# Turning gated blocks by a transposing DMA that reads from DRAM, in a fused retention and window-attention layer

## The chip, the cores and the metric

The kernel runs on one core of a Trainium2 chip. The metric is the device time of one execution in microseconds (us), the median of several runs. Besides the timed runs there is one execution with the hardware profiler on; its page and its trace are what this document reads. The granted TensorE clock was 1.000 over the whole profiled execution.

## What is computed

One decoder layer on x of 2048 tokens by 1024 channels, all in float32. One input projection makes 2816 columns; two groups of heads run side by side, their gated outputs are joined and projected back.

```python
h = rms_norm(x, norm_w)
proj = h @ w_in                              # 1024 -> 2816
rq, rk, rv, rg, sq, sk, sv, sg = split(proj) # r: retention, s: sliding window
ro = retention(rotary(rq), rotary(rk), rv)   # 4 heads, chunks of 128 tokens
ro = group_norm(ro) * ret_norm_w * silu(rg)  # 512 channels
so = sliding_window_attention(sq, sk, sv)    # 8 heads, 2 kv heads, window 128, sinks
so = so * silu(sg)                           # 512 channels
out = x + concat(ro, so) @ w_out             # 1024 -> 1024
```

The last product contracts over channels, so each gated output, which comes out of the retention with tokens on the partitions, has to be turned until channels are on the partitions before TensorE can use it. The change is about how that turn is made.

## The kernel before, in words

The 2048 tokens are 16 chunks of 128. Two neighbouring chunks, 2p (even) and 2p+1 (odd), are a pair p = 0 to 7. A gated output of one chunk is a block of 128 by 512 float32 (256 KB): n = 0 is the retention's, n = 1 the window attention's. The attention already comes out with channels on the partitions (its `so`), but its gate, which comes out of the input projection, has tokens there; so for n = 1 it is the gate that is turned, and for n = 0 the product of output and gate.

The four large products (three column ranges of the input projection, then the output projection) are done in a seven-product scheme on 2 by 2 blocks (`products`, line 672): for each pair p there are products numbered m = 1 to 7, each of 12 matmuls, because every float32 operand is split in two fp32r parts (`split`, line 494: ScalarE makes the high part, VectorE the low part) and three of the four partial products are kept over four blocks of the contraction. One product is one unit of the program's own time scale; a phase has 56 units, and the phases start at units 0, 56, 112 and 168. The order in a phase is `STEPS` (line 68): products 1 and 2 of all pairs, then 6, 5, 7 and 4, and 3 last.

The third phase yields the gates: for pair p its four results go to `gates` (line 1383). The retention's even chunk (row = col = 0) is the first of the four: its gate is stored to DRAM (`g_dram`) and loaded again at a unit set by `GATE` (line 1459). The other three go straight into `gate` (line 1346), which loads the stored output (`ro_dram` or `so_dram`) into a tile `go`, applies SiLU to the gate on ScalarE, and then, for n = 0, multiplies on VectorE, turns the product by four 128 by 128 transposes on TensorE (label "turn gated") and copies it from PSUM with ScalarE (label "mixed"). For n = 1 it multiplies the gate by the softmax denominators, turns the gate with `turn_by_dma` (line 1324), and multiplies it into `go` on VectorE.

`turn_by_dma` before: a transposing DMA moves 2-byte elements, so ScalarE first copies the float32 tile into a tile `apart` that holds all the first halves of the words and then all the second halves (one ACTIVATE over 1024 uint16 per partition). The DMA transposes `apart` into `turned`, from SBUF to SBUF. A second ScalarE copy (label "together") puts the halves of `turned` side by side again.

The result is `mixes[p, q]` with q = 0, 1 for the even chunk's n = 0, 1 and q = 2, 3 for the odd chunk's. The fourth phase's `blocks` (line 598, called in line 1449 with `p, q ^ 2`) takes the odd chunk's blocks for products 1 and 2 and all four of a pair from product 6 on, which comes 16 units later.

The order of the work is not written by hand. `Program` (line 135) is given every operation with its costs per engine, its operands and a due time in units, and `emit` (line 169) plays them through a model of the engines, of tile slots and of the one DMA queue, and emits each engine's instructions in the order in which the model starts them. That order is fixed per engine. A DMA waits in SP's queue for its inputs, with all that stands behind it. In the model a plain DMA of 256 KB holds the transfers for 0.70 us, lands 2.6 us later (`dma`, line 349), and what depends on a DMA may be queued on SP 0.06 + 0.8 us after that (`SEM`, `LATE`). So a change of a cost or a due time moves the order of other work too.

Every engine instruction is recorded at line 377, where a helper issues it; the groups in the views are told apart by the names of their tiles. In those names, from line 1346 on, `r` and `t` are the window attention's gates of odd and even chunks on their way, `s` the odd chunks' retention gates, `g` the even chunks', `go` is the tile that ends up as mixed block, `m` is a PSUM bank, `acc` the bank of a large product, `x` and `w` its operands, `res` a tile of x to be added to the result.

Of the kernel before, what the change touches and what calls it, by code (L numbers as in the profile page):

```python
# [29 lines left out]
F32 = mybir.dt.float32  # L30
# [279 lines left out]

LOG = None


def dve(n, two=False, lat=0.08):
    return (0.067 + n / 960, 0.067 + n / 960 + lat, two)
# [2 lines left out]
def act(n, more=0.0):  # L318
    return (0.094 + n / 1200 + more, 0.2 + n / 1200 + more, False)
# [6 lines left out]
def both(n):  # L326
    return {"V": dve(n, True)}
# [21 lines left out]
def dma(kb, issue=0.45):  # L349
    return {"Q": (0.45 + kb / 1024, 2.6, issue)}  # L350
# [30 lines left out]
def layer(ctx, tc, xt, xfirst, xtok, nw, w_in, w_rn, qkw, sinks, biasg, rope, dmask, gpow, w_out, out):  # L381
# [33 lines left out]
    def fixed(shape, name, dtype=F32):  # L415
        return Buf(name=name, ap=const.tile(shape, dtype, name=name))

    def scratch(shape, name, n):
        t = dram.tile([n, *shape], F32, name=name)
        return [Buf(name=name, ap=t[i]) for i in range(n)]  # L420

    def given(ap):
        return Buf(ap=ap)
# [398 lines left out]
    def retention(at):  # L822
# [4 lines left out]
        for c in range(NCH):  # L827
# [4 lines left out]
            load(a0, rq_dram[0][c], due - 3, 192, also=(a,))  # L832
            load(a1, rq_dram[1][c], due - 3, 64, also=(a,), of=lambda t: t[:, 0:128])
            load(rp, given(rope[c].rearrange("p s c -> p (s c)")), due - 3)
            load(v0, rq_dram[1][c], due - 3, 128, also=(v,), of=lambda t: t[:, 128:384])
            load(v1, aq_dram[1][c], due - 3, 128, also=(v,), of=lambda t: t[:, 256:512])
            for j, r in enumerate((rstd_all, rsq_all)):

                def go(e, rp=rp, j=j, r=r, c=c):
                    t = rp().rearrange("p (s c) -> p s c", s=2)[:, :, j * P : (j + 1) * P]  # L840
                    e.activation(t, t, AF.Copy, scale=r()[:, c : c + 1])

                op({"A": act(256, 0.09)}, go, [rp, r], [rp], due - 2, label="scale rope")

            tcos, tsin, qk = kb("tcos", "ret"), kb("tsin", "ret"), kb("qk", "ret")
            for i, t in enumerate((tcos, tsin)):

                def go(e, t=t, i=i, a=a, rp=rp):
                    h = "p (h c) -> p h c"
                    e.tensor_tensor(  # L850
                        t().rearrange(h, h=2),
                        a().rearrange(h, h=2),
                        rp().rearrange("p (s c) -> p s c", s=2)[:, i : i + 1, :].to_broadcast([P, 2, 256]),
                        ALU.mult,
                    )

                op(both(512), go, [a0, a1, rp], [t], due, label="rotary", also=(a,))

            for i, alu in enumerate((ALU.subtract, ALU.add)):

                def go(e, i=i, alu=alu, tcos=tcos, tsin=tsin, qk=qk):
                    r = "p (h a f) -> p h a f"
                    x, y = (tcos, tsin) if i == 0 else (tsin, tcos)
                    e.tensor_tensor(
                        qk().rearrange("p (a b f) -> p a b f", b=2, f=32)[:, :, i, :],
                        x().rearrange(r, h=2, f=32)[:, 0],
                        y().rearrange(r, h=2, f=32)[:, 1],
                        alu,
                    )

                op(both(256), go, [tcos, tsin], [qk], due + 0.1, label="rotary sum")

            pt, qkT = ps(), kb("qkT", "ret")

            def go(e, pt=pt, qk=qk):
                for i in range(4):
                    e.transpose(pt()[:, i * P : (i + 1) * P], qk()[:, i * P : (i + 1) * P], ident())

            op(turns(4), go, [qk, ident], [pt], due + 0.2, "small", label="turn qk")

            op({"A": act(512)}, lambda e, pt=pt, qkT=qkT: e.activation(qkT(), pt(), AF.Copy), [pt], [qkT], due + 0.3,
               label="qkT")
            halves = (slice(0, 64), slice(64, 128))


# [130 lines left out]
    def window(at):  # L1016
# [33 lines left out]
        for c in range(NCH):  # L1050
            i = c >= 2 * FIRST_PAIRS
            a, b = kb("aq", "att"), sb("akv", [P, P])
            load(a, aq_dram[0][c], at(c) - 4)
# [18 lines left out]
    def values(c, held, due, d, differences):  # L1072
# [22 lines left out]
        def go(e):  # L1095
# [9 lines left out]
            for u in range(4):  # L1105
                for g, r in enumerate((L, H)):
                    for k, rows in enumerate((L, H)):
# [4 lines left out]
                            start=False, stop=True, skip_group_check=True,  # L1112
                        )

        reads = [*parts, *differences, *held[0][0], *held[1][0], *held[0][2], *held[1][2]]
        op(f32(512, 3.2), go, reads, pavs, due + 2, "both", label="values", also=(n, s, d, *own))
        for k in range(2):
            so = kb("so", "att")
            op({"A": act(512)}, lambda e, so=so, k=k: e.activation(so(), pavs[k](), AF.Copy), [pavs[k]], [so], due + 2.1,
               label="so")  # L1120
            store(so_dram[c + k], so, due + 2.2)

    def qk_sums(p, row, col, b, due):

# [43 lines left out]
    def attend(c, a, b, fac, facs, due, bias_t, ks_t, nsnk, held):  # L1168
# [9 lines left out]
                ALU.mult,  # L1178
            )

        op(both(512), go, [a, facs], [qn], due, label="qn")

        def go(e):
            for g in range(KVH):
# [10 lines left out]
            label="turn k",  # L1195
        )

        def go(e):
            for i in range(4):
                e.transpose(pq()[:, i * P : (i + 1) * P], qn()[:, i * P : (i + 1) * P], ident())  # L1200

        op(turns(4), go, [qn, ident], [pq], due + 0.2, "small", label="turn q")
        qT = kb("qT", "att")

        def go(e):

# [4 lines left out]
            )  # L1211

        op({"A": act(256)}, go, [pk], [ks_t], due + 0.3, label="ks")
        op({"A": act(512)}, lambda e: e.activation(qT(), pq(), AF.Copy), [pq], [qT], due + 0.35, label="qT")

# [64 lines left out]
        for g in range(KVH):  # L1280
            pm, own = pms[g], owns[g]
            pp, pT = ps(), kb("pT", "att")

            def go(e, pp=pp, pm=pm):
                for j in range(GRP):
                    e.transpose(pp()[:, j * P : (j + 1) * P], pm()[:, j * P : (j + 1) * P], ident())

            op(
                turns(4), go, [*weights_of[g], *weights_of[2 + g], ident], [pp], due + 1.3 + 0.3 * g, "small",
                label="turn weights", also=(pm,),  # L1290
            )
            op({"A": act(512)}, lambda e, pT=pT, pp=pp: e.activation(pT(), pp(), AF.Copy), [pp], [pT], due + 1.4 + 0.3 * g,
               label="pT")
# [11 lines left out]
            op({"G": (0.61, 0.7, True)}, go, [pT], [part], due + 1.5 + 0.3 * g, label="own", also=(own,))  # L1305
            pTs.append(pT)
            own_parts.append(part)
        op(
# [11 lines left out]


    mixes = {}

    def turn_by_dma(t, due):


        apart, turned = kb("apart", "turned"), kb("turned", "turned")
        words = lambda x: x.bitcast(U16).rearrange("p (c h) -> p h c", h=2)
        planes = lambda x: x.bitcast(U16).rearrange("p (h c) -> p h c", h=2)
        op(  # L1330
            {"A": act(1024)}, lambda e: e.activation(planes(apart()), words(t()), AF.Copy), [t], [apart], due,
            label="apart",
        )
        op(
            {"Q": (1.4, 3.0, 0.45)},
            lambda e: e.dma_start_transpose(
                turned().bitcast(U16).rearrange("p (j r) -> p j r", r=P), apart().bitcast(U16)
            ),
            [apart], [turned], due, label="turn by dma",
        )  # L1340
        op(
            {"A": act(1024)}, lambda e: e.activation(words(t()), planes(turned()), AF.Copy), [turned], [t], due + 0.1,
            label="together",
        )

    def gate(n, c, due, g):

# [13 lines left out]
        else:  # L1361
# [94 lines left out]

WIN = (54.0, 5.6)
RET = (107.0, 2.8)
GATE = (150.0, 1.2)

LEAD = 12.0

# [95 lines left out]
```

## Time and profile before

| | us |
|---|---|
| median of 3 runs | 709.81 (709.15 to 710.41) |
| the profiled execution, its own time | 709.88 |
| its span, first to last instruction | 708.0 |
| TensorE matmuls busy (share of the span) | 702.2 (99%) |
| VectorE busy | 606.9 (86%) |
| ScalarE busy | 471.9 (67%) |

How to read the lines: PE is TensorE, DVE VectorE, ACT ScalarE, POOL GpSimd, SP the queue that issues nearly all DMAs. A group's line gives engine, operation, the tile written and the tiles read, shapes, the count, busy time, mean duration in nanoseconds, and the engine's idle time just before these instructions with what ended it. Matmuls overlap, so the duration of one (some 270 to 390 ns) is longer than the distance between two. A window's row gives length, then busy us and number of instructions of each engine, granted clock, mean busy share of the 16 DMA engines and GB/s; the DMA share can exceed 1 a little.

### The profile page before, as it was taken

How to read it: one execution, taken by the hardware profiler on the slowest of the kernel's cores; microseconds unless marked ns; L12 is line 12 of the kernel's file. 1: busy time of each engine (PE TensorE's matmuls, PEld its weight loads, DVE VectorE, ACT ScalarE, POOL GpSimd, SP SyncE). 2: the span in 40 equal slices, each digit the busy share in tenths (PEclk: the TensorE clock that was granted, in tenths of full speed). 3: DMA queues.
4: the chain of work that ended last, by engine and by line, in shares of the span. 5: the costliest groups of instructions: out<-in, count | busy, mean ns of one | idle time of the engine just before them, and what ended most of it. 6: DMA issues, size and time to landing. Idle time of an engine off the chain costs nothing.

```text
span 708.0 us, 15295 instructions
## 1 busy us (share of the span) xinstructions
PE 702.2 (99%) x5324; PEld 603.3 (85%) x5324; DVE 606.9 (86%) x1458; ACT 471.9 (67%) x1103; POOL 43.8 (6%) x75
## 2 busy tenths in 40 slices
PE   9999999999999999999999999999999999999998
PEld 7888888889999999998888888888888878888886
DVE  6999877877997977799999979998699989997862
ACT  7666966655795548788588667789999976250500
POOL 1000000025110001002001010000000000000000
PEclk9999999999999999999999999999999999999999
DMA  8978939968545557998977738292999951324722
GB/s 322 358 263 294 404 123 316 313 230 276 183 132 169 198 172 213 357 302 257 335 223 251 208 114 290 71 333 100 303 341 235 256 128 60 103 91 131 256 103 90
DMA packets 118924, 157.66 MB, mean 223 GB/s; under 512 B 28736, under 2 KB 57408, under 8 KB 118848
## 3 DMA queue, kind: packets, MB, share of 16 engines
q1 hardware_dynamic: 118704, 156.69, 67.5%
q8 instruction: 42, 0.69, 0.4%
q14 instruction: 34, 0.28, 0.1%
q10 hardware_dynamic: 144, 0.00, 0.0%
HBM read 110.44 MB, written 42.01 MB: 215 GB/s over the span
## 4 chain that ended last, share of the span: by engine, by line
PE 97%; DVE 2%; issue 0%; DMA 0%; SPq 0%; ACT 0%
PE acc L377 80%; PE m L377 17%; DVE w L377 1%; DVE x L377 1%; DVE t L377 0%; DMA res<-in_xtok 0%; DVE res L377 0%; DVE go L377 0%; SPq L377 0%; ACT x L377 0%; DVE none L377 0%
## 5 line engine op out<-in xcount | busy, mean ns | idle before, releaser
L377 PE MATMUL acc<-w,x 128*128 128x512 f32 (+1 forms) x2700 | 598.5, 378 | 1.1 <-DVE x L377 0.8
L377 PEld LDWEIGHTS acc<-w,x 128*128 128x128 f32 x2700 | 491.1, 188 | 82.0 <-issue 2.7
L377 DVE TENSOR_TENSOR x<-x 128x512 fp32r<-128x512 f32 (+2 forms) x220 | 145.4, 681 | 16.4 <-ACT x L377 15.9
L377 ACT ACTIVATE x<-x 128x512 fp32r<-128x512 f32 (+1 forms) x187 | 112.1, 617 | 7.0 <-DVE x L377 2.6
L377 ACT ACTIVATE w<-w 128x512 fp32r<-128x512 f32 (+1 forms) x72 | 41.2, 603 | 38.1 <-DMA w<-in_w_out 17.8
L377 DVE TENSOR_TENSOR w<-w 128x512 fp32r<-128x512 f32 (+3 forms) x96 | 62.5, 669 | 2.9 <-ACT w L377 2.9
L377 DVE TENSOR_TENSOR s<-acc,s 128x512 f32<-128x512 f32 (+1 forms) x64 | 42.0, 656 | 16.3 <-PE acc L377 15.8
L377 ACT ACTIVATE pm<-lg,nm 128x128 f32<-128x128 f32 x128 | 49.7, 392 | 6.8 <-DVE lg L377 6.8
L377 DVE CUSTOM_DVE_ANT_0 lg<-m,bias,nsnk 128x160 f32<-128x160 f32 x128 | 42.3, 381 | 10.1 <-PE m L377 10.0
L377 DVE SCALAR_TENSOR_TENSOR w<-w,nw_sb 128x512 fp32r<-128x512 f32 (+3 forms) x72 | 49.3, 706 | 0.9 <-ACT w L377 0.7
L377 POOL TENSOR_SCALAR_AFFINE_SELECT own<-pT 64x512 f32<-64x512 f32 x32 | 26.4, 837 | 291.7 <-ACT pT L377 246.5
L377 DVE TENSOR_TENSOR t<-acc,t 128x512 f32<-128x512 f32 (+2 forms) x33 | 21.1, 640 | 17.0 <-PE acc L377 16.6
L377 ACT ACTIVATE x<-go 128x512 fp32r<-128x512 f32 x40 | 24.0, 633 | 12.1 <-PE acc L377 6.3
L377 ACT ACTIVATE s<-acc 128x512 f32<-128x512 f32 (+1 forms) x32 | 18.2, 569 | 19.6 <-PE acc L377 14.7
L377 DVE TENSOR_TENSOR r<-acc,t 128x512 f32<-128x512 f32 (+1 forms) x32 | 21.0, 656 | 11.8 <-PE acc L377 11.4
L377 ACT ACTIVATE w<-w,nw_sb 128x512 fp32r<-128x512 f32 (+3 forms) x43 | 28.0, 681 | 2.7 <-DMA w<-in_w_in 2.7
L377 DVE TENSOR_TENSOR x<-go,x 128x512 fp32r<-128x512 f32 x40 | 27.2, 685 | 0.0
L377 ACT ACTIVATE ro<-ro,nmu,rg 128x128 f32<-128x128 f32 x64 | 25.1, 482 | 0.9 <-DVE nmu L377 0.9
L377 ACT ACTIVATE c<-acc 128x512 f32<-128x512 f32 (+1 forms) x24 | 13.4, 559 | 16.6 <-PE acc L377 13.9
L377 ACT ACTIVATION_READ_ACCUMULATOR pm<-lg,nm 128x1 f32 x128 | 24.4, 190 | 0.0
L377 DVE TENSOR_TENSOR t<-acc,s 128x512 f32<-128x512 f32 (+1 forms) x32 | 21.0, 656 | 3.3 <-PE acc L377 2.8
L377 ACT ACTIVATE xk<-xk 128x512 f32<-128x512 f32 x32 | 19.8, 620 | 5.3 <-DMA xk<-in_xtok 5.3
(133 smaller groups left out, 726.4 us busy)
## 6 DMA issues: line engine op xcount, KB each, us to landing
x<-in_xt SPq DMA_DIRECT2D x80, 256.0 KB, 5.0
x<-s_dram SPq DMA_DIRECT2D x64, 256.0 KB, 4.3
w<-in_w_in SPq DMA_DIRECT2D x40, 256.0 KB, 5.4
s_dram<-x SPq DMA_DIRECT2D x32, 256.0 KB, 5.0
xk<-in_xtok SPq DMA_DIRECT2D x32, 256.0 KB, 5.1
res<-in_xtok SPq DMA_DIRECT2D x32, 256.0 KB, 3.3
w<-in_w_out SPq DMA_DIRECT2D x20, 256.0 KB, 4.7
aq<-aq_dram SPq DMA_DIRECT2D x16, 256.0 KB, 4.8
```

The source lines that it names most:

```text
L377: return lambda *a, **k: self.order.put(op(*a, **k))
```

## The change

`turn_by_dma` takes another path. The halves of the words are put apart by ScalarE as before, but the tile `apart` is then stored to DRAM (a plain DMA of 256 KB), into a scratch where each token's 1024 halves are one row. The transposing DMA reads that scratch as 256 rows of 512 halves: row 2t holds the first halves of token t, row 2t + 1 the second halves. Turned, the two halves of a word lie side by side, so the tile it writes is already float32 and the copy "together" is gone. The tile that was put apart is itself the destination.

The even chunks' n = 0 blocks go this way too; the odd chunks' n = 0 blocks stay on TensorE. `GATE` moves from unit 150 with 1.2 units between pairs to unit 145 with 2.0. In the model a transposing DMA now costs (1.5, 3.0, 1.35) instead of (1.4, 3.0, 0.45): the last number is the time for which SP's queue is held. The other sets in `TURNED` are empty, so the branches for them (turning q, the retention's q and k, the attention weights) change no operation.

```diff
+TURN = (1.5, 3.0, 1.35)
+TURNED = {"q": (), "qk": (), "weights": (), "gated": range(0, NCH, 2)}
...
+    def turn_by_dma(t, to, planes, due, of=None, also=()):
+        apart = kb("apart", "turned")
+        op(
+            {"A": act(1024, 0.12)},
+            lambda e: e.activation(
+                apart().bitcast(U16).rearrange("p (h c) -> p h c", h=2),
+                t().bitcast(U16).rearrange("p (c h) -> p h c", h=2), AF.Copy,
+            ),
+            of or [t], [apart], due, label="apart", also=also,
+        )
+        store(planes, apart, due + 0.1, of=lambda t: t.bitcast(U16))
+        op(
+            {"Q": TURN},
+            lambda e: e.dma_start_transpose(
+                to().bitcast(U16).rearrange("p (j r) -> p j r", r=2 * P),
+                planes().rearrange("t (h c) -> (t h) c", h=2),
+            ),
+            [planes], [to], due + 0.2, label="turn by dma",
+        )
...
+    planes_dram = [scratch([P, 1024], f"planes{n}_dram", NCH, U16) for n in range(6)]
...
-    def turn_by_dma(t, due):
-        apart, turned = kb("apart", "turned"), kb("turned", "turned")
...
-            {"Q": (1.4, 3.0, 0.45)},
-            lambda e: e.dma_start_transpose(
-                turned().bitcast(U16).rearrange("p (j r) -> p j r", r=P), apart().bitcast(U16)
-            ),
...
-            {"A": act(1024)}, lambda e: e.activation(words(t()), planes(turned()), AF.Copy), [turned], [t], due + 0.1,
-            label="together",
...
-        if n == 0:
+        if n == 0 and c not in TURNED["gated"]:
             pm = ps()
...
         else:
-            turn_by_dma(g, due + 0.3)
+            t = (o, g)[n]
+            turn_by_dma(t, t, planes_dram[n][c], due + 0.3)
+        if n == 1:
             op(both(512), lambda e: e.tensor_tensor(o(), g(), o(), ALU.mult), [g, o], [o], due + 0.4, label="mixed")
...
-GATE = (150.0, 1.2)
+GATE = (145.0, 2.0)
```

More of the change, by code (lines that the diff above doesn't have):

```diff
@@ L831, in retention @@
             v0, v1 = (Part(v, lambda t, s=s: t[:, s]) for s in (slice(0, 256), slice(256, 512)))
[L832 to L834 removed]
+            soon = due - (EARLIER_K if c in TURNED["qk"] else 0)
+            load(a0, rq_dram[0][c], soon - 3, 192, also=(a,))
+            load(a1, rq_dram[1][c], soon - 3, 64, also=(a,), of=lambda t: t[:, 0:128])
+            load(rp, given(rope[c].rearrange("p s c -> p (s c)")), soon - 3)
             load(v0, rq_dram[1][c], due - 3, 128, also=(v,), of=lambda t: t[:, 128:384])
@@ L869, in go @@
                     )
-                op(both(256), go, [tcos, tsin], [qk], due + 0.1, label="rotary sum")
+                op(both(256), go, [tcos, tsin], [qk], soon + 0.1, label="rotary sum")
             pt, qkT = ps(), kb("qkT", "ret")
[L875 to L882, printed above, removed]
+            if c in TURNED["qk"]:
+                turn_by_dma(qk, qkT, planes_dram[3][c], soon + 0.1)
+            else:
+                def go(e, pt=pt, qk=qk):
+                    for i in range(4):
+                        e.transpose(pt()[:, i * P : (i + 1) * P], qk()[:, i * P : (i + 1) * P], ident())
+                op(turns(4), go, [qk, ident], [pt], due + 0.2, "small", label="turn qk")
+                op({"A": act(512)}, lambda e, pt=pt, qkT=qkT: e.activation(qkT(), pt(), AF.Copy), [pt], [qkT], due + 0.3,
+                   label="qkT")
             halves = (slice(0, 64), slice(64, 128))
@@ L1113, in go @@
                         )
+        late = due + (LATER_W if c in TURNED["weights"] else 0)
         reads = [*parts, *differences, *held[0][0], *held[1][0], *held[0][2], *held[1][2]]
-        op(f32(512, 3.2), go, reads, pavs, due + 2, "both", label="values", also=(n, s, d, *own))
+        op(f32(512, 3.2), go, reads, pavs, late + 2, "both", label="values", also=(n, s, d, *own))
         for k in range(2):
             so = kb("so", "att")
-            op({"A": act(512)}, lambda e, so=so, k=k: e.activation(so(), pavs[k](), AF.Copy), [pavs[k]], [so], due + 2.1,
+            op({"A": act(512)}, lambda e, so=so, k=k: e.activation(so(), pavs[k](), AF.Copy), [pavs[k]], [so], late + 2.1,
                label="so")
-            store(so_dram[c + k], so, due + 2.2)
+            store(so_dram[c + k], so, late + 2.2)
     def qk_sums(p, row, col, b, due):
@@ L1179, in go @@
             )
-        op(both(512), go, [a, facs], [qn], due, label="qn")
+        soon = due - (EARLIER_Q if c in TURNED["q"] else 0)
+        op(both(512), go, [a, facs], [qn], soon, label="qn")
         def go(e):
@@ L1196, in attend, with go @@
         )
[L1198 to L1202, printed above, removed]
         qT = kb("qT", "att")
+        if c in TURNED["q"]:
+            turn_by_dma(qn, qT, planes_dram[2][c], soon + 0.1)
+        else:
+            def go(e):
+                for i in range(4):
+                    e.transpose(pq()[:, i * P : (i + 1) * P], qn()[:, i * P : (i + 1) * P], ident())
+            op(turns(4), go, [qn, ident], [pq], due + 0.2, "small", label="turn q")
+            op({"A": act(512)}, lambda e: e.activation(qT(), pq(), AF.Copy), [pq], [qT], due + 0.35, label="qT")
         def go(e):
@@ L1282, in attend, with go @@
             pp, pT = ps(), kb("pT", "att")
[L1284 to L1293, printed above, removed]
+            if c in TURNED["weights"]:
+                turn_by_dma(pm, pT, planes_dram[4 + g][c], due + 1.3 + 0.3 * g, [*weights_of[g], *weights_of[2 + g]], (pm,))
+            else:
+                def go(e, pp=pp, pm=pm):
+                    for j in range(GRP):
+                        e.transpose(pp()[:, j * P : (j + 1) * P], pm()[:, j * P : (j + 1) * P], ident())
+                op(
+                    turns(4), go, [*weights_of[g], *weights_of[2 + g], ident], [pp], due + 1.3 + 0.3 * g, "small",
+                    label="turn weights", also=(pm,),
+                )
+                op({"A": act(512)}, lambda e, pT=pT, pp=pp: e.activation(pT(), pp(), AF.Copy), [pp], [pT], due + 1.4 + 0.3 * g,
+                   label="pT")
             r = (L, H)[slot]
@@ L1303, in go @@
                 )
-            op({"G": (0.61, 0.7, True)}, go, [pT], [part], due + 1.5 + 0.3 * g, label="own", also=(own,))
+            op({"G": (0.61, 0.7, True)}, go, [pT], [part], due + 1.5 + 0.3 * g + (LATER_W if c in TURNED["weights"] else 0), label="own", also=(own,))
             pTs.append(pT)
```

23 lines of the change are left out of this document (6 added, 17 removed).

## The prediction, made before the change was run

> **What bounds the kernel now.** I read the busy shares of the page first, then its chain of waits, then a table of windows over the stretch in which gated blocks are made, and last that stretch instruction by instruction on each engine.
>
> ```profile
> span 708.0 us, 15295 instructions
> ...
> PE 702.2 (99%) x5324; PEld 603.3 (85%) x5324; DVE 606.9 (86%) x1458; ACT 471.9 (67%) x1103; POOL 43.8 (6%) x75
> ...
> PE 97%; DVE 2%; issue 0%; DMA 0%; SPq 0%; ACT 0%
> ```
>
> TensorE has something to do in all but 5.8 of 708.0 us, and the chain that ended last is TensorE for 97%. An instruction taken off TensorE therefore comes off the time, as long as nothing else is late where it stood. The windows say how near the others are.
>
> ```profile
> 440.00:460.00 20.00, 20.00 (x167) 16.78 (x165) 18.37 (x54) 15.01 (x36) 1.44 (x2) 1.00 0.33 102
> 460.00:480.00 20.00, 20.00 (x156) 16.64 (x141) 20.00 (x58) 17.24 (x34) 0.00 (x0) 1.00 0.96 336
> 480.00:500.00 20.00, 20.00 (x243) 17.09 (x242) 14.39 (x47) 19.53 (x47) 1.45 (x2) 1.00 0.30 98
> 500.00:540.00 40.00, 40.00 (x200) 33.27 (x199) 33.64 (x55) 39.16 (x65) 0.00 (x0) 1.00 1.08 341
> 540.00:580.00 40.00, 39.73 (x180) 32.25 (x179) 36.97 (x62) 38.85 (x53) 0.00 (x0) 1.00 0.77 186
> ```
>
> ScalarE, 67% busy over the span, is busy for 78.0 of the 80 us from 500 to 580, VectorE for 70.6, and the DMA engines are full from 500 to 540. That stretch, not the averages, is what the change has to be weighed in.
>
> **The turns taken off TensorE.** These rows of the chain show four turns, the product behind them, and a pair of turn groups ahead of four undisturbed products.
>
> ```profile
> 502.78 0.44 PE m L377 x4
> 503.22 2.76 PE acc L377 x12
> ...
> 522.37 0.87 PE m L377 x8
> 523.24 10.90 PE acc L377 x48
> ```
>
> ```profile
> L377 PE MATMUL m<-ident,go 128*128 128x128 f32 x64 | 9.1, 272 | 0.0
> ```
>
> The 64 turns are 16 chunks by four; the even chunks' 32 go. Four cost 0.44 us on the chain (eight cost 0.87; the mean of 272 ns is one turn's length with overlap, not its distance to the next). So 8 × 0.44 = 3.5 us come off. A product behind a turn takes 2.76 us against 10.90 / 4 = 2.73, which would add 8 × 0.03 = 0.2 us; I leave that to the lower end.
>
> The Trainium skill speaks against this: "VectorE: DVE Perf Modes", in "The three transpose paths", has 390 ns for a 128×128 bf16 transpose on TensorE and 1309 ns by DMA, and its "Rules for kernel authors" choose TensorE where the result may land in PSUM. Two bytes at a time, a block is eight such tiles, so by the page it would take about 10.5 us by DMA, an estimate; the measured landing below is shorter, and what the rule would do here is the third rival.
>
> **What ScalarE loses and gets.**
>
> ```profile
> L377 ACT ACTIVATE go<-m 128x512 f32<-128x512 f32 x16 | 9.3, 608 | 0.7 <-PE m L377 0.5
> L377 ACT ACTIVATE r<-turned 128x1024 uint16<-128x1024 uint16 x8 | 11.3, 1407 | 0.1
> L377 ACT ACTIVATE t<-turned 128x1024 uint16<-128x1024 uint16 x8 | 11.1, 1387 | 0.0
> L377 ACT ACTIVATE apart<-r 128x1024 uint16<-128x1024 uint16 x8 | 8.4, 1067 | 0.1
> ```
>
> All 16 copies "together" go (11.3 + 11.1 = 22.4 us), and half of the copies out of PSUM (9.3 / 2 = 4.7). Eight more copies "apart" come (8 × 1.07 = 8.5). Net ScalarE is relieved of 18.6 us, nearly all of it between 480 and 580 where it has none to spare. On the path that is worth only what TensorE waits there for it, which is next. VectorE's work doesn't change.
>
> ```profile
> 565.70 3.17 ACT L377 ACTIVATE apart<-t 128x1024 uint16<-128x1024 uint16 x3
> ...
> 576.60 1.38 ACT L377 ACTIVATE t<-turned 128x1024 uint16<-128x1024 uint16 x1
> ```
>
> ```profile
> 572.12 9.26 PE L377 MATMUL acc<-w,x 128*128 128x512 f32 x38 [0.22 <-ACT x L377]
> 582.17 18.20 PE L377 MATMUL acc<-w,x 128*128 128x512 f32 x79 [0.80 <-DVE x L377]
> ```
>
> The last blocks of the window attention are put apart at 565.7 to 568.9, put together up to 578, and only then multiplied and split for product 6 of the last phase. There TensorE loses 0.22 and 0.80 us, and its 38 matmuls took 9.26 us where 38 × 10.90 / 48 = 8.63 would do: 1.65 us in all. VectorE had added up the last of these gates much earlier:
>
> ```profile
> L377 DVE TENSOR_TENSOR t<-acc,t x4: 682/684/685, 540.6 to 550.2; 128x512 f32<-128x512 f32 x4
> ```
>
> They then wait some 15 us for ScalarE, so with 18.6 us less on ScalarE they should come sooner. But each also takes longer to land (next part). Bounds: 1.65 us gained, or 2.7 lost (the second rival). I take half of the loss as gained, 0.8, the nearer row being ScalarE without a gap before 569.
>
> **What DMA and SP get.** The first two rows are from the list of all DMA issues, the next three from that of 500 to 540, the last two from the views of single tiles.
>
> ```profile
> so_dram<-so SPq DMA_DIRECT2D x16, 256.0 KB, 4.1
> ...
> turned<-apart SPq DMA_TRANSPOSE x16, 4.4
> ```
>
> ```profile
> x<-s_dram SPq DMA_DIRECT2D x8, 256.0 KB, 5.1
> ...
> ro_dram<-ro SPq DMA_DIRECT2D x3, 256.0 KB, 5.9
> ...
> turned<-apart SPq DMA_TRANSPOSE x7, 5.1
> ```
>
> ```profile
> L377 SPq DMA_DIRECT2D so_dram<-so x16: 319/320/1247, 205.4 to 496.9; - x16
> L377 SPq DMA_TRANSPOSE turned<-apart x16: 1232/1321/1889, 508.6 to 571.3; - x16
> ```
>
> There come 24 stores of 256 KB and 8 more transposing DMAs. On SP's queue that is 24 × 0.32 + 8 × 1.32 = 18 us of issuing within 140 us. A transposing DMA that reads DRAM and writes words is not in this trace; its issue lies between that of a plain DMA (0.32) and twice the one seen (2.64), and I take 1.32, the same instruction on as many bytes. On the DMA engines 256 KB at 341 GB/s is 0.77 us, so 32 × 0.77 = 25 us. From 440 to 580 they have 140 − (0.33 + 0.96 + 0.30) × 20 − (1.08 + 0.77) × 40 = 34 us free, most of it before 500 and after 540. The even chunks, now due from unit 145, two units apart, fall largely into the free part before 500. I cost the traffic at nothing, the cover being how early x is loaded:
>
> ```profile
> 522.42 0.32 SPq L377 DMA_DIRECT2D x<-s_dram  x1
> ```
>
> ```profile
> 538.55 0.67 ACT L377 ACTIVATE x<-x 128x512 fp32r<-128x512 f32 x1
> ```
>
> The third phase's last operand is issued 16.1 us before ScalarE first reads it; less 5.1 to land, 11 us of delay are covered. Without that cover, each microsecond of delay would be one of TensorE's.
>
> The way of an even chunk's block grows to 1.07 + 4.1 + 4.4 = 9.6 us, where a turn and a copy out of PSUM took about one. It is first needed for product 6 of the last phase, prepared from unit 180 on; the last even chunk is due at 159, and 21 units of 2.73 us are 57 us. A window-attention block grows by 4.1 for the store less 1.4 for "together": 2.7 us; that one has no such cover at the end.
>
> **The sum** is made against the profiled execution's own 709.88 us, which stands 0.07 above the median of the runs: 709.88 − 3.5 − 0.8 = 705.6 us. The same differences hold for the median. About 0.2% (1.4 us) is the least that a measurement of this kernel can tell from no change.
>
> **The rivals.** First, VectorE becomes the bound. It keeps all its work and is busy for 36.97 of the 40 us from 540 on; if TensorE comes 3.5 us sooner and VectorE can't, TensorE waits for the difference at the start of product 6. Against it: VectorE is idle 6.4 us between 500 and 540 and 3.0 between 540 and 580, waiting behind a full ScalarE. Time: all of 3.5 given back, 709.9, or near it. Chance 0.10.
>
> Second, the longer way of the last window-attention blocks. If the copies "apart" come no earlier than now, product 6 is 2.7 us later: 709.88 − 3.5 + 2.7 = 709.1. For it speaks that the chain at 576 already waits on a transposing DMA:
>
> ```profile
> 576.62 0.69 DVE L377 TENSOR_TENSOR x<-x,go 128x512 f32<-128x512 f32 x1 [1.87 <-DMA turned<-apart]
> ```
>
> Against it, the relief of ScalarE; it decides only if those copies move forward by less than 2.7 us. Chance 0.12.
>
> Third, and slower: SP's queue is held. Each transposing DMA now waits in that queue for a store to land in DRAM, and loads of x and w_out stand behind it. The program's model queues it 0.70 + 2.6 + 0.06 + 0.8 = 4.2 us after the store; stores between 500 and 540 took 5.9, so SP may be held 1.7 us each time. The stretch now has 7 of 16, so I count 10 of the 24; they hold it 17 us; 11 are covered by the early loads, 6 are not: 709.88 − 3.5 + 6 = 712.4. It makes the kernel slower from a hold of 1.6 us per turn on (10 × 1.6 − 11 = 5, which is 3.5 and the 1.4 of the measurement). Against it speaks the one pair of store and dependent load that is there now, the 16 blocks stored to and loaded from `ro_dram`:
>
> ```profile
> SPq L377 <- DMA ro_dram<-ro: 2.1, 6, 0.9
> ```
>
> That is 0.13 us each. Chance 0.16, as the model's new order may also put them worse than I can see. The Trainium skill ("DMA: Bandwidth & Descriptors", "Latency and other measured facts") puts HBM's access at 0.2 us, but 2 us under high load; the growth from 4.1 to 5.9 us agrees with it, and by it this rival would weigh more the fuller the DMA engines are. If a transposing DMA out of DRAM holds SP for 2.64 us, that only adds to this case.
>
> That the change doesn't do what it says is hardly open: the 32 turns and 16 copies are gone by the code.
>
> **How the numbers follow.** The forecast, 705.6, has 0.62; its own range is 703.2 to 707.2: below, all 1.65 us regained, the 0.2 behind the turns, and as much again as the boundary's loss where the new order falls better elsewhere (709.88 − 3.5 − 1.65 − 0.2 − 1.3); above, a loss at the boundary 0.8 larger than now. The first two rivals end at 709.1 to 709.9 and the third at 712.4. A range from 703.2 to 710.2 takes in forecast and first two rivals and leaves out the third and a little of the forecast's lower tail, 2 in 10 at most. Faster by over 0.2% (below 708.4): the forecast and a quarter of the first two rivals, 0.68. Within 0.2%: most of these two, 0.16. Slower: the third, 0.16.
>
> **What would show it.** Right: 32 turns of `go` on TensorE, TensorE busy near 698.7 us; ScalarE busy near 453; no "together"; stores to the new scratch landing in 4 to 6 us; 24 transposing DMAs of about 1.3 us; SP's wait for those stores under 10 us in all; TensorE's gap ahead of product 6 smaller than 1 us. Wrong: TensorE idle beyond 6 us in all with VectorE (first rival) or a transposing DMA (second) as releaser after 560, or a late load of x between 480 and 545 (third).

## The result and the profile after

| | before | after |
|---|---|---|
| median of the runs on one chip (4 each) | 709.48 us (708.97 to 710.41) | 703.68 us (703.31 to 704.56) |
| after / before, 95% interval | | 0.9919, 0.9901 to 0.9936 |
| the profiled execution, its own time | 709.88 us | 703.66 us |
| its span | 708.0 us | 701.7 us |

The kernel became faster by 5.8 us, against 4.3 forecast; the interval of the ratio is 4.5 to 7.0 us. The page of the changed kernel, in the lines that answer to those shown of before:

```profile
span 701.7 us, 15257 instructions
...
PE 697.0 (99%) x5292; PEld 599.9 (85%) x5292; DVE 603.9 (86%) x1458; ACT 454.9 (65%) x1087; POOL 43.1 (6%) x75
...
PE 99%; DVE 0%; issue 0%
...
planes_dram<-apart SPq DMA_DIRECT2D x24, 256.0 KB, 5.2
```

TensorE's 32 instructions are gone and on balance 16 of ScalarE's (16 copies "together" and 8 out of PSUM went, 8 copies "apart" came); ScalarE is relieved by 17.0 us (471.9 − 454.9; 18.6 were forecast), and the chain that ended last went from 97% to 99% TensorE. TensorE is now idle for 4.7 us of the span instead of 5.8. The groups of the changed kernel:

```profile
L384 ACT ACTIVATE apart<-go 128x1024 uint16<-128x1024 uint16 x8 | 8.4, 1051 | 2.5 <-DVE go L384 1.5 <-ACT x L384 0.9
...
L384 PE MATMUL m<-ident,go 128*128 128x128 f32 x32 | 4.8, 271 | 0.0
L384 ACT ACTIVATE go<-m 128x512 f32<-128x512 f32 x8 | 4.7, 587 | 1.6 <-PE m L384 1.6
```

The same windows as before, a row each (length, then busy us and number of instructions of PE, PEld, DVE, ACT and POOL, clock, DMA share, GB/s):

```profile
440.00:460.00 20.00, 20.00 (x183) 16.73 (x186) 18.29 (x58) 16.99 (x36) 1.44 (x2) 1.00 0.53 161
460.00:480.00 20.00, 20.00 (x141) 16.42 (x133) 18.91 (x53) 17.83 (x33) 0.00 (x0) 1.00 0.78 241
480.00:500.00 20.00, 20.00 (x185) 17.28 (x178) 17.23 (x52) 16.39 (x33) 0.00 (x0) 1.00 1.04 290
500.00:540.00 40.00, 40.00 (x244) 33.01 (x243) 30.67 (x53) 37.25 (x73) 1.45 (x2) 1.00 1.05 320
540.00:580.00 40.00, 40.00 (x182) 33.12 (x181) 37.12 (x62) 26.20 (x41) 0.00 (x0) 1.00 1.11 299
```

From 540 to 580 ScalarE is busy for 26.20 us instead of 38.85. The DMA engines, which were full for 40 us, are now full for the 100 us from 480 to 580, and TensorE has no gap in any of these rows. Its timeline shows where the rest of the gain lies:

```profile
550.59 0.60 PE L384 MATMUL m<-ident,go 128*128 128x128 f32 x4
550.95 49.26 PE L384 MATMUL acc<-w,x 128*128 128x512 f32 x216
```

These are the last turns and the matmuls behind them, up to 600 us, where the stretch shown ends: the two gaps of before, at 572 and 582, aren't there. One row of the chain, the long run of matmuls in the first phase, first of before and then of after, shows a difference that isn't the change's, since it stands ahead of everything that was edited:

```profile
5.04 151.22 PE acc L377 x663
```

```profile
5.04 150.40 PE acc L384 x663
```

So the 6.3 us between the two spans divide as follows.

- 0.8 us stand in the first phase already (151.22 − 150.40): a difference between two executions. In the other kernels below, the same 663 matmuls take 150.5 to 151.1 us, whatever was edited.
- The matmuls behind the last turns begin at 550.95 instead of 555.31, 4.36 us sooner; less the 0.82, 3.5 us fall between the first phase and that point. Eight groups of turns lie there.
- From that point to the end it takes 701.7 − 550.95 = 150.75 us instead of 708.0 − 555.31 = 152.69, so 1.9 us more are gained: the loss ahead of product 6, 1.65 us, forecast at half its size, and 0.3 besides.

On the medians the last two, 5.4 us, stand against 5.8.

### The profile page after: what moved, and what is told of

Read it like the earlier page. It is cut to its first block, busy times and chain, and to the rows that moved or that the text cites. A ratio compares the mean times of both kernels' runs of the same rounds, so it can differ in the third digit from the quotient of the medians.

```text
span 701.7 us, 15257 instructions
## 1 busy us (share of the span) xinstructions
PE 697.0 (99%) x5292; PEld 599.9 (85%) x5292; DVE 603.9 (86%) x1458; ACT 454.9 (65%) x1087; POOL 43.1 (6%) x75
## 4 chain that ended last, share of the span: by engine, by line
PE 99%; DVE 0%; issue 0%
PE acc L384 83%; PE m L384 17%; DVE t L384 0%; DVE none L384 0%
## 5 line engine op out<-in xcount | busy, mean ns | idle before, releaser
L384 DVE TENSOR_TENSOR t<-acc,t 128x512 f32<-128x512 f32 (+2 forms) x33 | 21.1, 638 | 16.0 <-PE acc L384 15.9
```

What stands on the lines that cost most here:

```text
L384: return lambda *a, **k: self.order.put(op(*a, **k))
```

## The experiments

Three theories were to be told apart: that the gain is TensorE's time (the turns) and the end of the loss ahead of product 6; that one of the two would be there without the new path; and the rivals, above all SP's queue and the model's order. Each kernel is the changed one with the edit shown, unless the text says otherwise, and its ratio is against the kernel before on the same chip. The runs were made on several chips, on which the kernel before had medians from 709.40 to 710.02 us. So where two kernels of different chips are compared, their medians can mislead by some 0.6 us, and the difference of the two ratios is given beside that of the medians.

**The new path without the even chunks.** The 16 window-attention gates go over DRAM; the even chunks' blocks stay on TensorE, with the old due times.

```diff
-TURNED = {"q": (), "qk": (), "weights": (), "gated": range(0, NCH, 2)}
+TURNED = {"q": (), "qk": (), "weights": (), "gated": ()}
-GATE = (145.0, 2.0)
+GATE = (150.0, 1.2)
```

> The new path for the window attention's 16 gates alone: no even chunk of the retention is turned by DMA, and GATE is back at (150, 1.2). Theory: the change has two gains, 3.6 us from 32 turns taken off TensorE and about 1.9 us from the end of the loss ahead of product 6 of the last phase, and the second comes from ScalarE, which no longer puts the halves together (22.4 us less). Then this kernel keeps the second gain only: 709.5 - 1.9 = 707.6 us, 64 turns on TensorE, no wait of TensorE before product 6. Rival one (the second gain comes from the even chunks leaving, or from the earlier gates): no gain, 709.5 us. Rival two (the longer way over DRAM makes the last gates late): 2.7 us slower, 712.2 us.

Measured: 707.56 us (707.44 to 708.28), ratio 0.9967 (0.9955 to 0.9979). The path by itself is worth some 2.3 us, and TensorE's view of waits, which had two entries on `x` in the kernel before (the 0.22 and the 0.80 us), has none left in this kernel, only a wait of the first microseconds:

```profile
PE m L384 <- DVE none L384: 1.3, 1, 1.3
```

So the loss at product 6 goes with the new way of the 16 gates and the order that the model makes for it, and the step from here to the changed kernel, 707.56 − 703.68 = 3.9 us (3.4 by the ratios), with the even chunks.

**The even chunks by the old path.** All 24 blocks by the transposing DMA from SBUF to SBUF, with the second copy on ScalarE.

```diff
-        store(planes, apart, due + 0.1, of=lambda t: t.bitcast(U16))
+        turned = kb("turned", "turned")
...
+        op(
+            {"A": act(1024, 0.4)},
...
+            [turned], [to], due + 0.1, label="together",
+        )
```

> The changed kernel with the old path: the same 24 blocks are turned by DMA, but from SBUF to SBUF with the second copy on ScalarE, which the model now prices at its measured length; GATE stays at (145, 2.0). TensorE has the same 32 turns less. Theory: ScalarE gets 24 copies of 1.38 us more than the changed kernel, 33 us in a stretch where the kernel before had 2 us of 80 free, so product 6 waits: between 709 and 721 us, with a wait of TensorE for x after 560 of 5 us or more. Rival (what counts is only the turns off TensorE, ScalarE is covered): 703.7 to 705.9 us.

Measured: 724.12 us (722.83 to 725.43), ratio 1.0197 (1.0184 to 1.0211), with waits of TensorE for ScalarE's `x` of 11.0 us in all. That is slower by far, and above the range expected, but not a clean answer: in this kernel the last of the attention's exponentials (the tile `pm`), which start at 484.6 us in the kernel before, start at 584.0, so a second thing had moved as well.

**The old due times alone.**

```diff
-GATE = (145.0, 2.0)
+GATE = (150.0, 1.2)
```

> The changed kernel with GATE back at (150, 1.2). Theory: where the gates of the even chunks stand matters little, because they are needed 57 us later: within 0.7 us of the changed kernel, 703.0 to 704.4. Rival (the earlier gates spread the DMAs into the free stretch before 500 us, and without that the DMA engines or SP delay x): 705.6 us or more, with waits of TensorE between 500 and 580.

Measured: 709.27 us (706.94 to 710.93, 12 runs), ratio 0.9989 (0.9978 to 0.9999). This missed: nearly the whole gain is gone, by a due time that I had costed at nothing. Its execution in the profile, one of the faster ones (707.63), has the two gaps again:

```profile
588.88 0.73 PE L384 MATMUL acc<-w,x 128*128 128x512 f32 x2 [1.34 <-ACT x L384]
590.63 9.60 PE L384 MATMUL acc<-w,x 128*128 128x512 f32 x41 [1.01 <-DVE x L384]
```

The tile `pm`, of the kernel before, of the changed one and of this one (duration min/median/max in ns, first and last start in us), shows what else had moved:

```profile
L377 ACT ACTIVATE pm<-lg,nm x128: 384/388/426, 177.5 to 484.6; 128x128 f32<-128x128 f32 x128
```

```profile
L384 ACT ACTIVATE pm<-lg,nm x128: 384/388/423, 176.7 to 500.9; 128x128 f32<-128x128 f32 x128
```

```profile
L384 ACT ACTIVATE pm<-lg,nm x128: 384/390/422, 176.8 to 564.3; 128x128 f32<-128x128 f32 x128
```

The exponentials of the last attention chunk run at 561 to 564 us, behind gates whose SiLU needs ScalarE's other table. All that follows from them (the attention's values, its stores, the copies into `x`) comes late with them. The table load ahead of them is at 557.42 here; in the changed kernel it is at 496.89. The model counts a change of table as a cost, and with the old due times it finds no cheaper place for it. That was a theory at this point; the second set of runs tests it.

**All 16 chunks over DRAM.**

```diff
-TURNED = {"q": (), "qk": (), "weights": (), "gated": range(0, NCH, 2)}
+TURNED = {"q": (), "qk": (), "weights": (), "gated": range(NCH)}
```

> The changed kernel with the odd chunks' blocks of the retention turned by DMA too, so that no gated block is turned on TensorE. Theory, if DMA and SP have room: 3.6 us more, 700.1 us. Rival: the odd chunks' blocks are the first operands of the last phase, and the DMA engines are full from 480 to 580 us in the changed kernel (busy share 1.04 to 1.11), so TensorE waits at the start of the last phase and the gain is gone: 703.7 us or more.

Measured: 714.35 us (710.42 to 715.98), ratio 1.0046 (1.0026 to 1.0065). Slower than before, but the last exponentials start at 545.0 here, so this one is confounded too.

**The exponentials held in their place.** From here on each kernel has one more edit: the SiLU of the gates also reads the last chunk's softmax denominators, so that it can't be ordered ahead of the last exponentials. "Exps first" stands for it below.

```diff
-            [g, rstd_all], [g], due - 1, "silu", label="silu",
+            [g, rstd_all, rden_all[NCH - 1]], [g], due - 1, "silu", label="silu",
```

> The changed kernel with one dependency more in the model: no SiLU starts before the softmax of the last attention chunk is done, so ScalarE changes its function table once instead of three times after the start, and the last chunk's exponentials come at about 465 us instead of 497. Theory now: ScalarE's table change is what decides when the model lets the last chunk's exponentials run (480 us before, 497 in the changed kernel, 541 to 579 in the three runs that were slower than expected), and a last chunk after about 540 is late for the last phase. In the changed kernel it isn't late, so here: the same time, 703.7 +- 1 us, with two table loads (2.6 us of ScalarE) less. Rival: the earlier attention work pushes the gates back, 705 us or more.

Measured: 703.85 us (703.53 to 704.80), ratio 0.9921 (0.9907 to 0.9936). The last exponentials start at 466.4, there are two table loads fewer, and the time is that of the changed kernel. In the changed kernel, then, their place at 501 costs nothing.

**The old due times with exps first.**

```diff
-            [g, rstd_all], [g], due - 1, "silu", label="silu",
+            [g, rstd_all, rden_all[NCH - 1]], [g], due - 1, "silu", label="silu",
...
-GATE = (145.0, 2.0)
+GATE = (150.0, 1.2)
```

> The run with GATE at (150, 1.2) and the same added dependency. Theory: GATE mattered only through the place of the last exponentials; with that place held, 703.7 +- 1 us, as the changed kernel. Rival (GATE matters by itself, by spreading the DMAs into the stretch before 500): 706 us or more, as without the dependency (709.3).

Measured: 703.39 us (703.29 to 704.28), ratio 0.9915 (0.9900 to 0.9929). The 5.9 us between this kernel and the one with the old due times alone (5.3 by the ratios) are the place of the exponentials. `GATE` matters through nothing else that these runs can see. It is the lowest median of the study and can't be told from the changed kernel's.

**The old path for 24 blocks, exps first.**

```diff
-        store(planes, apart, due + 0.1, of=lambda t: t.bitcast(U16))
+        turned = kb("turned", "turned")
...
+            [turned], [to], due + 0.1, label="together",
...
-            [g, rstd_all], [g], due - 1, "silu", label="silu",
+            [g, rstd_all, rden_all[NCH - 1]], [g], due - 1, "silu", label="silu",
```

> The 24 blocks turned by the old path, from SBUF to SBUF with the second copy on ScalarE, and the same added dependency. Theory: ScalarE still has 33 us more than in the changed kernel where it has little to spare, so TensorE waits for x in the last phase: 710 to 718 us, with ScalarE as releaser. Rival (the slowness of the old path, 724 us, was the late last chunk alone): 703.7 to 705.5 us.

Measured: 718.13 us (717.85 to 718.68), ratio 1.0121 (1.0106 to 1.0135), 14.3 us above the same kernel with the new path. Its window and its view of waits:

```profile
540.00:580.00 40.00, 32.26 (x129) 24.88 (x129) 33.72 (x55) 37.34 (x50) 0.00 (x0) 0.91 0.89 218
```

```profile
PE acc L384 <- ACT x L384: 6.0, 2, 3.9
PE acc L384 <- DVE x L384: 3.5, 3, 1.8
```

ScalarE is nearly full where TensorE now waits. So the two parts of the change belong together: turning the even chunks by DMA pays only if the second copy is gone.

**All 16 chunks, exps first.**

```diff
-TURNED = {"q": (), "qk": (), "weights": (), "gated": range(0, NCH, 2)}
+TURNED = {"q": (), "qk": (), "weights": (), "gated": range(NCH)}
...
-            [g, rstd_all], [g], due - 1, "silu", label="silu",
+            [g, rstd_all, rden_all[NCH - 1]], [g], due - 1, "silu", label="silu",
```

> All 32 gated blocks turned by DMA, with the same added dependency. Theory one (the late last chunk alone spoiled this): 703.7 - 3.6 = 700.1 us. Rival (the DMA engines and SP are full, the first blocks of the last phase come late over DRAM): 706 us or more, with a wait of TensorE between 530 and 545 as in the run without the dependency (4.2 us).

Measured: 720.46 us (718.36 to 721.65), ratio 1.0149 (1.0129 to 1.0170). The exponentials are early and the kernel is slower still, so late exponentials weren't what made all chunks slow. The place expected for the wait was wrong too: between 530 and 545 TensorE waits 0.65 us, not 4.2. It waits for weights later, the chain goes through a store and a load behind it, and SP's queue shows why the load is late:

```profile
PE acc L384 <- DVE w L384: 4.8, 4, 2.3
PE acc L384 <- ACT w L384: 4.3, 3, 2.7
```

```profile
589.24 5.25 DMA planes_dram<-apart
...
594.55 5.35 DMA w<-in_w_out
```

```profile
580.51 2.12 SPq L384 DMA_TRANSPOSE r<-planes_dram  x1
582.72 2.96 SPq L384 DMA_TRANSPOSE t<-planes_dram  x1
...
589.76 5.59 SPq L384 DMA_DIRECT2D w<-in_w_out  x6
```

Two transposing DMAs hold the queue for 5.1 us. Then it is at six loads of `w` for 5.59 us, because ahead of the last of them it waits 2.4 us for the store begun at 589.24 to land, and that load ends the chain. Before, the last loads of this batch were issued by 561.1 us, in the changed kernel by 575.6, here at 595.0. This is the third rival in kind: SP's queue, held by the way over DRAM, makes the loads behind it late. But SP waits for stores to the scratch only 4.4 us in all here, so the hold that the rival counted is one part at most; the transposing DMAs' own time on the queue is another, and how the loss divides between them isn't shown. With 32 blocks the kernel is 16.6 us slower than with 24 (720.46 − 703.85), and of the 12.7 us for which TensorE waits in all, 9.1 are for `w`.

**The kernel before with exps first.** This puts the rival that the second gain isn't the new path's. The dependency goes into the kernel before; its slots for the tiles apart and turned go from 6 to 8 with it.

```diff
-            [g, rstd_all], [g], due - 1, "silu", label="silu",
+            [g, rstd_all, rden_all[NCH - 1]], [g], due - 1, "silu", label="silu",
```

> The kernel before with the added dependency (no SiLU before the last chunk's softmax) and 8 instead of 6 tiles for turning, without which the model finds no order. It tells how much of a gain the dependency alone can give. Theory: the last chunk is not late in the kernel before, ScalarE's two table loads less (2.6 us) are small beside the 22.4 us of second copies: 709.4 +- 1 us. Rival (the dependency, not the DMA path, is what helps): 705 us or less.

Measured: 707.52 us (706.94 to 708.93), ratio 0.9969 (0.9957 to 0.9980). This missed too. The loss ahead of product 6 is gone here as well, without any new path, although ScalarE remains nearly full (39.01 of 40 us):

```profile
540.00:580.00 40.00, 40.00 (x186) 33.15 (x186) 36.93 (x61) 39.01 (x59) 0.00 (x0) 1.00 1.00 244
```

So neither the new path nor the relief of ScalarE is needed for that gain; another order of the work is enough. The dependency and the two slots came together, and which of them did it wasn't separated.

**32 idle turns.** The changed kernel with exps first, and the even chunks' products turned on TensorE as well, into a PSUM bank that nothing reads. It computes the same output and does that much idle work.

```diff
+            if n == 0:
+                pm = ps()
+
+                def go(e):
+                    for i in range(4):
+                        e.transpose(pm()[:, i * P : (i + 1) * P], o()[:, i * P : (i + 1) * P], ident())
+
+                op(turns(4), go, [o, ident], [pm], due + 0.3, "small", label="idle turns")
```

> The changed kernel with the added dependency, and with the 32 transposes of the even chunks put back on TensorE as idle work: they write a PSUM bank that nobody reads, and the blocks still go by DMA. Theory: the turns cost what they cost on the chain, 8 x 0.44 us: 703.85 + 3.5 = 707.4 us. Rival (the gain of the even chunks is one of order, not of TensorE's time): 703.9 us.

Measured: 707.66 us (707.08 to 708.80), ratio 0.9971 (0.9959 to 0.9982): 3.8 us above the kernel without them (3.5 by the ratios). The first gain is TensorE's time: putting 32 turns back, with the DMA path left as it is, takes it all away.

**Two more blocks over DRAM.** Chunks 13 and 15 too, exps first.

```diff
-TURNED = {"q": (), "qk": (), "weights": (), "gated": range(0, NCH, 2)}
+TURNED = {"q": (), "qk": (), "weights": (), "gated": (*range(0, NCH, 2), 13, 15)}
```

> The changed kernel with the added dependency and two odd chunks more turned by DMA, 13 and 15, whose blocks the last phase needs latest. Theory: 8 x 0.11 = 0.9 us less for TensorE, 703.0 us, if SP and the DMA engines still have room for two blocks. Rival (the room ends near the changed kernel's 24 blocks; 32 cost 16.6 us): 704.5 us or more, with loads of w_out late.

Measured: 705.20 us (705.10 to 705.88), ratio 0.9936 (0.9922 to 0.9949). Two blocks more cost 1.35 us (1.1 by the ratios, whose intervals still overlap) instead of gaining 0.9:

```profile
591.58 20.28 PE L384 MATMUL acc<-w,x 128*128 128x512 f32 x88 [0.53 <-DVE w L384]
613.22 12.08 PE L384 MATMUL acc<-w,x 128*128 128x512 f32 x52 [1.35 <-DVE x L384]
```

The first wait is for `w` again, whose last load of that batch is issued at 580.5, against 576.0 with 24 blocks and exps first. The second and longer wait is for VectorE, which has had no gap from 579.83 to 613.2. In the kernel with 24 blocks and exps first VectorE has no gap there either, from 575 to 614, and yet TensorE never waits for it. SP waits for stores to the scratch 2.2 us in all here, and 2.0 us with 24 blocks. So the gain ends between 24 and 26 blocks at these places, but that SP's queue is what ends it isn't shown.

**24 idle copies on ScalarE.** The new path with exps first, and behind each copy "apart" a second copy of 1024 halves into a tile that nothing reads, as idle work beside the same output. It has the old path's copies without the old path.

```diff
...
+            e.activation(
+                idle().bitcast(U16).rearrange("p (c h) -> p h c", h=2),
+                apart().bitcast(U16).rearrange("p (h c) -> p h c", h=2), AF.Copy,
+            )
...
```

> The changed kernel with the added dependency, and with one idle copy of 1024 halves on ScalarE behind each of the 24 copies apart; nobody reads its result, so no block waits for it except through ScalarE. Theory (the old path's price is ScalarE's time): like the old path with the same dependency, 712 to 719 us, with TensorE waiting for x after 550. Rival (its price is the second copy's place in the way of each block): 703.9 to 705 us.

Measured: 718.88 us (717.85 to 719.22), ratio 1.0123 (1.0110 to 1.0137), within 0.8 us of the old path's 718.13. A block doesn't wait for the idle copy itself: one store to the scratch is issued at 541.61 us, when the idle copy of the same tile starts, too. What the old path costs at 24 blocks is ScalarE's time for the second copy, and not the DMA from SBUF to SBUF.

## Why the prediction was right, point by point

**What bounds the kernel.** Right: what came off TensorE came off the time.

**The turns, 3.5 us.** Right in kind and size: 3.5 us between the traces, 3.8 us in the run with idle turns, 3.9 us between the new path alone and the changed kernel (3.5 and 3.4 by the ratios).

**The loss ahead of product 6.** Right in sign, and the term of the sum that was mis-sized: I took half of 1.65 us, 0.8, and 1.9 came. That is all of it and 0.3 more. The choice of half was a middle between two bounds, so that the sum came as near as it did is partly luck. ScalarE's copies came earlier, as expected; before and after, last starts at the end of the range of times:

```profile
L377 ACT ACTIVATE apart<-t x8: 1042/1078/1117, 533.3 to 567.8; 128x1024 uint16<-128x1024 uint16 x8
```

```profile
L384 ACT ACTIVATE apart<-t x8: 1042/1050/1072, 534.9 to 559.3; 128x1024 uint16<-128x1024 uint16 x8
```

They came forward by 8.5 us, three times the 2.7 us by which each block's way was to grow. But the reason that I gave, that these copies on ScalarE held up product 6, isn't seen in the chain of before. It leads to the two waits like this:

```profile
571.56 0.69 DVE w L377
572.25 0.61 DVE x L377
...
572.90 7.81 PE acc L377 x33
...
580.74 0.64 ACT x L377
...
581.43 0.70 DVE x L377
```

At the first wait, 0.22 us were for a copy to `x` on ScalarE, which had stood idle for 0.83 us just before; the matmuls behind it then waited for VectorE, which had had no gap since 555.59 us and did eight operations on `w` between 555.6 and 572.2. The second wait ended with a copy to `x` on ScalarE and its other half on VectorE. There, too, ScalarE wasn't busy ahead of the copy: it stood idle for 0.35 us until TensorE was done with an earlier product. So a change of order could end this loss with ScalarE nearly full, as the kernel before with exps first shows. The sign was right; the mechanism behind it was at best one way to the gain.

**DMA and SP at nothing.** Right for 24 blocks, and not far from the edge. The hold of SP's queue by a store, disputed between 0.13 and 1.7 us, is this row of SP's waits (total, times, longest):

```profile
SPq L384 <- DMA planes_dram<-apart: 9.8, 12, 3.3
```

That is 9.8 / 24 = 0.41 us per turn, a quarter of the 1.6 us at which the third rival would have decided. The landing of the stores from 500 to 540, 5.0 us, was within the 4 to 6 named. The transposing DMA out of DRAM, costed at 1.32 us, takes about that on SP:

```profile
L384 SPq DMA_TRANSPOSE go<-planes_dram x8: 1233/1427/2460, 456.8 to 527.8; - x8
```

It lands in 5.1 to 5.5 us. The estimate of 10.5 us that I had worked out from the Trainium skill ("VectorE: DVE Perf Modes", "The three transpose paths") is twice that. The preference of the Trainium skill for TensorE ("VectorE: DVE Perf Modes", "Rules for kernel authors") doesn't hold here, where TensorE is the engine that is full and 32 turns cost it some 3.5 us.

**GATE at nothing.** Wrong as a step, though not in the sum. I looked at when the even chunks' blocks are needed and not at what else the due time moves. Through the model's order it moved the last exponentials by 63 us (501 to 564), and with the old value 5.6 us of the gain are gone (709.27 − 703.68; 5.0 by the ratios).

**The rivals.** VectorE didn't become the bound at 24 blocks (37.12 us busy of 40, no gap of TensorE); at 26 the longer of the two waits was for it, though it is as full with 24. The longer way of the last blocks decided nothing, as the copies came forward. SP's queue did not decide at 24 blocks; at 32 it stands in the chain, though not by the waits for stores alone; at 26 its part isn't shown.

**What stays open.** Why the loss at product 6 goes away in the kernel before with exps first, where ScalarE is as full as it was and the last copy "apart" comes at 573.9, later than before. Only the order of the work there differs; which step of it decides wasn't isolated. One lead: from 555.6 to 572.2 us VectorE is busy for 15.9 to 16.6 us of 16.6 in the four kernels that follow, but does eight operations on `w` in the kernel before, five in the kernel before with exps first, four with the new path alone and two in the changed kernel. Putting `w` behind the operands of product 6, with nothing else moved, would test it.

## What to carry to other kernels

When one engine is full all along, moving its small jobs to a path that is slower for each of them pays, as long as no other queue on that path becomes late; so ask first which engine gives the second half of the path its time (here a copy on ScalarE had to go before the DMA path could carry the even chunks). Where a scheduler with a cost model orders the work, a due time isn't a local edit: look where the operations that share a costly mode, here ScalarE's table, end up in the new order. And find the edge before adding more of a good thing: here eight blocks gained some 3.5 us, two on top of them gave 1.1 to 1.35 back, and eight on top made the kernel 11 us slower than before.

## What the runs showed of the hardware

**A long wait of TensorE costs more than itself.** In the run with idle copies on ScalarE, TensorE waits 2.83 and 5.22 us, and the 12 matmuls behind each take about 5 us instead of 2.73:

```profile
554.60 4.88 PE L384 MATMUL acc<-w,x 128*128 128x512 f32 x12 [2.83 <-ACT x L384]
564.70 5.08 PE L384 MATMUL acc<-w,x 128*128 128x512 f32 x12 [5.22 <-ACT x L384]
```

```profile
555.00:560.00 5.00, 4.47 (x12) 2.94 (x10) 4.97 (x9) 3.91 (x6) 0.00 (x0) 0.66 0.99 235
560.00:565.00 5.00, 0.30 (x1) 0.31 (x2) 4.39 (x8) 4.97 (x8) 0.00 (x0) 0.73 0.46 149
565.00:570.00 5.00, 4.78 (x12) 3.33 (x11) 2.45 (x5) 4.94 (x6) 0.00 (x0) 0.58 0.92 248
```

The granted clock of these windows is 0.58 to 0.73, and TensorE's busy time grew to 703.0 us from 697.3 with the same 5292 matmuls. So of the 15 us lost there some 6 stand as busy time at the lower clock, not as waits. The Trainium skill ("TensorE: Matmul & The Clock Gate", "What's actually happening") puts the clock at half after an idle window of some 3.4 us; the trace agrees with about half (4.88 / 2.73 = 1.8), and shows it behind a wait of 2.83 us already. Behind the waits of 0.53 and 1.35 us in the run with two more blocks the matmuls kept their pace (52 in 12.08 us, which is 2.79 for 12).

**Full DMA engines are no loss by themselves.** They stood at a share of 1.04 to 1.11 for 100 us while TensorE never waited; with 32 blocks, TensorE waited mostly for `w` (9.1 of 12.7 us), whose loads had been issued late on SP's queue.
